# Nine steps of fill products moved from the end of the delta rule's scan to the second group's gram products

## The chip, the cores and the metric

The kernel runs on one core of a Trainium2 chip, as one launch. The metric is the device time of that launch in microseconds (us): the median of three executions is 1509.61 us (1508.7 to 1509.68).

A core has five engines that run side by side, each through its own list of instructions in a fixed order: TensorE (PE in the profile; its weight loads are PEld), VectorE (DVE), ScalarE (ACT), GpSimd (POOL), and SyncE (SP), which here issues most of the transfers (DMAs). An instruction waits on semaphores until what it needs is there, and everything behind it on the same engine waits with it.

## The reference, cut to what matters

One layer works on 512 latent tokens and 256 context tokens of width 1024: a feed-forward block, then two mixers side by side (neighbourhood attention and a gated delta rule, forward and backward over 768 tokens), merged by gates, then a second feed-forward block. The part around the change is the delta rule and the projections of the same normalized input:

```python
qa, ka, va, qkv_b, z_b, a_b, b_b, ga, gb = split_proj(modulate(x, shift_x, scale_x) @ w_in)
...
m = jnp.where(strict, jnp.einsum('...ik,...jk->...ij', k_beta, k) * decay, 0.0)
uw = lax.linalg.triangular_solve(jnp.eye(GDN_CHUNK, dtype=m.dtype) + m, rhs,
                                 left_side=True, lower=True, unit_diagonal=True)
...
def step(s, xc):
    v_new = xc[0] - jnp.einsum('...ck,...kv->...cv', xc[1], s)
    s_next = s * xc[3][..., None, None] + jnp.einsum('...ck,...cv->...kv', xc[2], v_new)
    return s_next, (jnp.einsum('...ck,...kv->...cv', xc[4], s)
                    + jnp.einsum('...cj,...jv->...cv', xc[5], v_new))
```

A unit triangular system per chunk has to be inverted, and a state runs through the chunks in order. The projections qa, ka, va (the attention's) and ga, gb (the merge gates) depend on none of that.

## The kernel before

**The delta rule** works in chunks of 128 tokens: six chunks, each in two directions for four heads. One scan position `s` (0 to 5) holds one forward and one backward chunk; `p` (0 or 1) is a pair of heads. So one call works on four 128x128 blocks: two directions by two heads. The positions go in three groups `bi` of two (s = 0,1; 2,3; 4,5).

For each group:

- `grams(bi)` calls `gram(p, s, ...)` four times. It loads decay rows (`Dt<-gcd`, L1110), subtracts and adds a mask on DVE (L1113), takes the exponential on ACT (L1114), lets PE multiply k by k (and q by k from s = 2 on) in `products` (tile `pq`, recorded at L1049, the line of `mm`), and makes `Bt` (DVE, L1119) and `At` (DVE, L1123). `Bt` goes to memory (`bd<-Bt`, L1120).
- `base_inverse` reads 32x32 diagonal blocks of `bd` back into `L` (`Ltr<-bd` and `L<-bd`, L1139; a copy on ACT, L1140; a memset on POOL, L1142) and inverts all of them at once, 31 pairs of a product and a sum on DVE (`bt`, L1146, and `Xt`, L1147). It writes `rd<-Xt` (L1151). There is one buffer `L`, so the base inverses of the three groups follow each other.
- `inverse(bi, st, ...)` loads `T<-rd` (L1168), transposes it on DVE (L1170, L1171) and joins the blocks to 64 and 128 with small matmuls (tile `pi`).
- `scan_step(p, s, ...)` runs the state: matmuls into `pc` (S by kT, r by Tt, vn by ktail, S by qT, vn by At), with DVE between them (`r`, `vn`, `S`, `otmp`), and additions into `oacc` on POOL (L1289, L1290) for s = 4, 5.

`gdn_out(p)` at the end squares `oacc` on ACT, sums on DVE, takes a root on POOL, scales on DVE (L1303), transposes on PE (L1052) and writes `obd`. Then comes the neighbourhood attention, head pair by head pair (`attend`): scores `sc` (L1433), softmax on DVE and ACT (`pr`, L1441), transposes `pt` (L1448), their copy `pT` on ACT (L1450), and the product with the values (L1459).

**The fills** are 28 products of a 1024x128 weight with the 512 tokens, for qa, ka, va, ga and gb (`FILLS`). Each is cut into FS = 4 steps of six matmuls 128x512 (a weight in a high and a low part: L192, L193, L194, tile `pm`); the last step also copies the result on ACT (`spill`) and sends it to memory (L802). The weight comes by DMA on SP's queue (`wr`, L174), is cast on ACT (`wh`, L137) and its rest is taken on DVE (`wl`, L139). `turn(kind, i)` adds `RATE[kind][i]` to a counter and issues one step for each whole unit, behind the last matmul recorded so far: kind "g" after a gram product, "i" within an inverse, "s" within a scan step, `i` being the group. Before the first gram product stand N0 * FS = 8 steps. After the scan a loop issues steps until `(len(FILLS) - NLATE) * FS` are reached and the last product is whole; what is left is issued behind the first attention head (`for _ in fills`).

**The order on each engine** isn't the order of the program text alone. The kernel is built with `schedule_with_timeline_sim=True`: a planner simulates the engines and puts in the instruction whose inputs are there in its simulation, earlier program text first. A fill step is tied behind one matmul, but a step outside `turn` isn't, and may be drawn forward. On the chip the planned order is fixed, and the times are the chip's.

The order of the program text around the change:

```python
for _ in range(N0 * FS):
    next(fills)
step(grams(0))
base = grams(1)
inv_of(0, 0)
...
while done[0] < (len(FILLS) - NLATE) * FS or done[0] % FS:
    next(fills)
```

Of the kernel before, what the change touches and what calls it, by code (L numbers as in the profile page):

```python
# [58 lines left out]
def body(ctx, tc, I, out, dbg=None):  # L59
# [4 lines left out]
    def pool(name, side="left", space=None):  # L64
        kw = dict(name=name, bufs=1, reuse_waits="tile")
        if space is not None:
            kw["space"] = space
        else:
            kw["side"] = side
        g = tc.tile_pool(**kw)  # L70
        st = ExitStack()
        p = st.enter_context(g)
        return p, st.close
# [492 lines left out]
    g = []  # L566
# [472 lines left out]
    gq, close_gq = pool("gq")  # L1039
    spool, done = [gq], [0]  # L1040
    gb_, close_gb = pool("gbase", "right")
    FS, N0, NKQ, NLATE = 4, 2, 2, 3
    RATE = {"g": (2, 3.9, 0.7), "i": (1.5, 0, 0), "s": (0.7, 0.9, 0.5)}
    NBT, NAT, NT6, NTT = 8, 8, 1, 2

    last = [None]
# [17 lines left out]
    def turn(kind, i):  # L1064

        due[0] += RATE[kind][i]
        while due[0] >= 1:
# [837 lines left out]
```

## Time and profile before

| | before |
|---|---|
| median of 3 executions | 1509.61 us |
| the profiled execution: its own time | 1512.61 us |
| its span in the trace | 1510.8 us |
| PE busy | 1441.6 us (95%) |
| DVE busy | 1149.5 us (76%) |
| ACT busy | 662.8 us (44%) |
| POOL busy | 211.2 us (14%) |
| granted TensorE clock, mean | 0.986 |

The profile is one execution. Times within it run from the start of its span. "Busy" is the time in which an engine has an instruction at work; matmuls are pipelined and their ends are modelled, so the step from one start to the next says more of PE's rate than the length of one. The granted clock is the share of full speed that PE got. In a row of the timeline stand the start, the length, the engine, the line, the operation, the tiles (out<-in), the shapes and the count; in brackets the idle time before it, and what ended that. In the chain of waits each piece is what the next one waited for. The gram products, inverses and scan of the delta rule lie between about 736 and 980 us, and the first attention head follows.

### The profile page before, as it was taken

The numbers are of one execution on the slowest core, as the hardware profiler recorded it, in microseconds if no ns is written. First come the engines' busy times: TensorE is split into PE (matmuls) and PEld (weight loads), VectorE is DVE, ScalarE is ACT, GpSimd is POOL, SyncE is SP. The second block draws the span as 40 slices with busy tenths as digits, with TensorE's granted clock in tenths as the row PEclk, the third lists the DMA queues.
The fourth block names the chain that finished last, engine by engine and source line by source line (L and its number), as shares of the span: only waits on it lengthen the run. The fifth ranks groups of instructions, "written<-read, shape, count | busy, mean of one in ns | idle before, by whom it ended". The sixth has DMA issues, their size and how long they took to land.

```text
span 1510.8 us, 23895 instructions
## 1 busy us (share of the span) xinstructions
PE 1441.6 (95%) x9117; PEld 1262.9 (84%) x9117; DVE 1149.5 (76%) x1975; ACT 662.8 (44%) x1090; POOL 211.2 (14%) x262
## 2 busy tenths in 40 slices
PE   6998999999999989999996998989999999999997
PEld 4778989999997778889875777867778999998886
DVE  8787869999988665778677795567669699886626
ACT  5433524434333386555534334267526454444310
POOL 1000000000000110313201001333221022220001
PEclk9999999999999999999998999999999999999999
DMA  9677664445469444222576514274344143233732
GB/s 375 207 262 232 209 236 171 156 164 167 165 231 397 157 153 134 92 78 91 175 214 183 168 64 124 72 261 146 100 168 144 60 136 107 98 112 121 269 98 83
DMA packets 114948, 248.56 MB, mean 165 GB/s; under 512 B 35145, under 2 KB 50577, under 8 KB 114833
## 3 DMA queue, kind: packets, MB, share of 16 engines
q1 hardware_dynamic: 110192, 229.40, 45.4%
q0 software_dynamic: 3056, 12.33, 2.2%
q10 hardware_dynamic: 1586, 5.32, 0.9%
q8 instruction: 71, 1.16, 0.3%
q14 instruction: 43, 0.35, 0.1%
HBM read 215.50 MB, written 31.50 MB: 163 GB/s over the span
## 4 chain that ended last, share of the span: by engine, by line
PE 69%; DVE 13%; DMA 10%; issue 4%; ACT 3%; POOL 1%; SPq 1%; DVEq 0%; ACTq 0%; POOLq 0%
PE ps L211 15%; PE ps L533 4%; PE ps L535 4%; PE ps L534 4%; PE pm L192 4%; PE pm L193 4%; PE pm L194 4%; PE ps L193 3%; PE ps L192 3%; PE ps L1679 3%; PE ps L194 3%; PE ps L1680 3%; PE ps L1681 3%; PE pc L1049 2%; DVE wl L139 2%
## 5 line engine op out<-in xcount | busy, mean ns | idle before, releaser
L139 DVE TENSOR_TENSOR wl<-wr,wh 128x1024 fp32r<-128x1024 f32 (+1 forms) x184 | 226.8, 1238 | 119.2 <-ACT wh L137 119.0
L137 ACT CAST wh<-wr 128x1024 fp32r<-128x1024 f32 (+1 forms) x184 | 185.9, 1015 | 265.7 <-PE pm L193 60.1
L192 PE MATMUL pm<-uxh,wh 128*128 128x512 f32 x320 | 132.4, 414 | 1.0 <-ACT spill L798 1.0
L194 PE MATMUL pm<-uxh,wl 128*128 128x512 f32 x320 | 127.2, 397 | 0.3 <-DVE wl L139 0.3
L193 PE MATMUL pm<-uxl,wh 128*128 128x512 f32 x320 | 127.1, 397 | 0.0
L211 PE MATMUL ps<-wh,hx 128*128 128x512 f32 x352 | 96.1, 391 | 0.9 <-ACT wh L137 0.9
L211 PEld LDWEIGHTS ps<-wh,hx 128*128 128x128 f32 x352 | 65.9, 188 | 15.3 <-ACT wh L137 1.3
L280 DVE SCALAR_TENSOR_TENSOR adap<-wr,crow 128x1024 f32<-128x1024 f32 x61 | 74.6, 1223 | 2.3 <-DMA wr<-in_w_adaT_dram 1.7
L192 PE MATMUL ps<-uh,wh 128*128 128x256 f32 (+1 forms) x208 | 68.6, 331 | 5.0 <-ACT wh L137 5.0
L194 PEld LDWEIGHTS pm<-uxh,wl 128*128 128x128 f32 x320 | 61.1, 191 | 14.3 <-DVE wl L139 1.3
L192 PEld LDWEIGHTS pm<-uxh,wh 128*128 128x128 f32 x320 | 61.5, 192 | 12.6 <-ACT spill L798 1.4
L193 PEld LDWEIGHTS pm<-uxl,wh 128*128 128x128 f32 x320 | 61.4, 192 | 10.6
L114 POOL TENSOR_TENSOR rs<-ve,mhalf 128x1 f32<-128x1 f32 (+2 forms) x46 | 48.2, 1050 | 140.7 <-DVE ve L110 138.3
L193 PE MATMUL ps<-ul,wh 128*128 128x256 f32 (+1 forms) x208 | 67.5, 326 | 0.0
L194 PE MATMUL ps<-uh,wl 128*128 128x256 f32 (+1 forms) x208 | 66.6, 325 | 0.0
L193 PE MATMUL ps<-uxl,wh 128*128 128x256 f32 (+1 forms) x192 | 61.6, 324 | 2.1 <-DVE uxl L139 2.1
L192 PE MATMUL ps<-uxh,wh 128*128 128x256 f32 (+1 forms) x192 | 60.7, 323 | 1.6 <-ACT uxh L137 1.4
L194 PE MATMUL ps<-uxh,wl 128*128 128x256 f32 (+1 forms) x192 | 61.1, 321 | 0.0
L137 ACT CAST wh<-ra 128x1024 fp32r<-128x1024 f32 x31 | 32.6, 1053 | 58.1 <-PE ps L534 20.2
L533 PE MATMUL ps<-ur,wh 128*128 128x384 f32 x168 | 56.5, 336 | 0.0
L534 PE MATMUL ps<-ur,wh 128*128 128x384 f32 x168 | 56.4, 336 | 0.0
L533 PE MATMUL ps<-uh,wh 128*128 128x384 f32 x168 | 56.4, 336 | 0.0
(498 smaller groups left out, 4264.4 us busy)
## 6 DMA issues: line engine op xcount, KB each, us to landing
wr<-in_w_adaT_dram SPq DMA_DIRECT2D x64, 512.0 KB, 4.8
wr<-in_up_dram SPq DMA_DIRECT2D x56, 512.0 KB, 3.7
wr<-in_win_dram SPq DMA_DIRECT2D x52, 512.0 KB, 3.4
wr<-in_dn_dram SPq DMA_DIRECT2D x51, 512.0 KB, 4.0
ra<-in_up_dram SPq DMA_DIRECT2D x24, 512.0 KB, 4.2
rb<-in_up_dram SPq DMA_DIRECT2D x18, 512.0 KB, 3.3
ra<-in_w_adaT_dram SPq DMA_DIRECT2D x16, 512.0 KB, 5.0
wr<-in_w_o_dram SPq DMA_DIRECT2D x8, 512.0 KB, 4.5
```

Source lines behind the costliest of these rows:

```text
L114: G.tensor_tensor(rs[:], ve[:], mhalf[:, 0:n], ALU.pow)
L137: S.copy(hi, src)
L139: marks["lo"] = V.tensor_tensor(lo, src, hi.bitcast(F32), ALU.subtract).ins
L192: T.matmul(ps, a, uh[:, k, :], start=(k == 0), stop=False)
L193: T.matmul(ps, a, ul[:, k, :], start=False, stop=False)
L194: marks["mm"] = T.matmul(ps, b, uh[:, k, :], start=False, stop=(k == nk - 1)).ins
L211: T.matmul(banks[t][d][:, c0:c1], a[:, sl], b[:, d * 512 + c0:d * 512 + c1], start=first and j == 0, stop=last and j == 2)
L280: V.scalar_tensor_tensor(pr[:], raw[:], 1.0, crow, op0=ALU.mult, op1=ALU.mult, accum_out=col[:, c:c + 1])
L533: T.matmul(ps[:], a, mh, start=k == 0, stop=False)
L534: T.matmul(ps[:], a, ml, start=False, stop=False)
L535: T.matmul(ps[:], b, mh, start=False, stop=k == 3)
L1679: T.matmul(ps[:], a, uh[:, k], start=k == 0, stop=False)
```

## The change

Two constants change. The rate of fill steps after a gram product of the second group goes from 3.9 to 5 for each of its eight turns, and the number of products that may be left for later goes from 3 to 2. No operation is added or removed; steps of the fill list are issued at other places of the program text.

```diff
-    FS, N0, NKQ, NLATE = 4, 2, 2, 3
-    RATE = {"g": (2, 3.9, 0.7), "i": (1.5, 0, 0), "s": (0.7, 0.9, 0.5)}
+    FS, N0, NKQ, NLATE = 4, 2, 2, 2
+    RATE = {"g": (2, 5, 0.7), "i": (1.5, 0, 0), "s": (0.7, 0.9, 0.5)}
```

## The prediction

> **What bounds the kernel now.** I read the busy time of every engine by stretches first, then TensorE's timeline around the stretch in which it is empty, then the waits and the chain of waits, to see what ended that emptiness. The question is where TensorE (PE) is empty, and whether work moved into one empty place leaves another behind.
>
> ```profile
> 800.50:804.00 3.50, 0.01 (x1) 0.00 (x0) 2.06 (x3) 1.95 (x1) 0.00 (x0) 1.00 0.74 209
> 804.00:808.00 4.00, 0.00 (x0) 0.00 (x0) 1.97 (x10) 0.63 (x1) 0.15 (x1) 0.69 0.83 147
> 808.00:812.50 4.50, 0.00 (x0) 0.00 (x0) 2.45 (x14) 0.00 (x0) 1.01 (x5) 0.50 0.99 263
> 812.50:816.00 3.50, 3.46 (x46) 2.46 (x50) 3.35 (x15) 1.86 (x5) 2.81 (x6) 0.54 0.17 52
> 816.00:819.50 3.50, 3.50 (x74) 2.69 (x76) 3.34 (x9) 1.29 (x2) 0.80 (x2) 1.00 0.48 155
> ```
>
> The columns are the stretch, its length, then busy time and instructions of PE, its weight load, VectorE (DVE), ScalarE (ACT) and GpSimd (POOL), the granted clock, the DMA share and GB/s. PE has nothing from 800.5 to 812.5 us, and the clock it gets falls to 0.50 and is still 0.54 up to 816.
>
> ```profile
> 794.81 0.48 PE L192 MATMUL pm<-uxh,wh 128*128 128x512 f32 x1
> 800.12 0.39 PE L194 MATMUL pm<-uxh,wl 128*128 128x512 f32 x1
> 812.54 0.69 PE L1049 MATMUL pi<-T,Bt 32*32 32x32 f32 x32 [12.04 <-DMA T<-rd]
> PE pi L1049 <- DMA T<-rd: 15.2, 3, 12.0
> 800.78 0.70 DVE Xt L1147
> 802.90 4.11 SPq L1151 DMA_DIRECT2D rd<-Xt  x4
> 808.76 3.43 DMA T<-rd
> ```
>
> The first two rows are the first and the last of the 24 matmuls behind the second group's last gram product, then comes the first inverse, 12.04 us after. Of all PE's waits in the scan this is the largest (12.0 of the 15.2 us that PE spent on T<-rd). What it waits for is told by the last rows, of the chain and of SP's queue: DVE ends the first base inverse at 801.48, Xt goes out to memory, and T comes back by 812.19. So 10.7 us of that hole is a round trip that no matmul can shorten; PE can only be given something to do meanwhile.
>
> **What the change does to the order.** The NLATE part does nothing. The loop behind the scan runs until done reaches (28-NLATE)*4 and is a multiple of 4. Counting the due counter through the code, the turns have made 101 steps by then before the change and 110 after: both lie past 100, and both values of NLATE lead to 104 before and 112 after. What acts is the rate 3.9 to 5 on eight turns: they issue 3,4,4,4,4,4,4,4 steps before and eight times 5 after, so 47 become 56 by the first inverse: nine steps more, of six matmuls each. All turns behind it issue the same number as before, each nine steps further on in the list. What is missing at the end is one step of the loop (3 become 2) and all 8 steps, two products, that stood behind the first attention head.
>
> **The front.** Nine steps are 54 matmuls. The two rows above give (800.12-794.81)/23 = 0.231 us from one to the next, so 12.5 us. PE's fills then end at 800.51+12.5 = 813.0 instead of 800.51, and the first inverse starts 0.5 later than 812.54 if T is there by then. In return there is no cold start: in 812.50 to 816.00 PE worked 3.46 us at 0.54, which at full clock is 1.9, so 1.6 us come back. The front is worth **-1.1**.
>
> The moved steps bring their own work along: 2.25 weights, each with a load of 512 KB in SP's queue, a cast on ACT, a split on DVE and a spill at its end.
>
> ```profile
> 795.16 1.22 DVE L139 TENSOR_TENSOR wl<-wr,wh 128x1024 fp32r<-128x1024 f32 x1
> 787.65 1.05 PE L1049 MATMUL pq<-kT 128*128 128x128 f32 x8
> 793.64 1.12 DVE L1119 SCALAR_TENSOR_TENSOR Bt<-pq,beta,Dt 128x128 f32<-128x128 f32 x4
> 799.46 0.68 DVE At L1123
> ```
>
> The splits are 2.25 x 1.22 = 2.7 us on DVE ahead of the end of the first base inverse. Against it, the last Bt and At (1.12 and 0.68) move behind that end, since their products come later. Between +2.7 and -1.8 on T I take 0: PE arrives at 813.0 and T at 812.2, so 0.8 of it is covered anyway, and the rest costs PE one for one. The loads and spills pass the same queue as rd and T; their density per PE time does not change, only its length, so I take 0 there too.
>
> **The second base inverse.** The last Bt of the second group waits for a product that now has seven more steps in front of it: 7 x 6 x 0.231 = 9.7 us, from 788.70 to 798.4. Behind that Bt are its way to memory, the loads of L, ACT's copy, and the second base inverse.
>
> ```profile
> 801.76 1.95 ACT L1140 COPY L<-Ltr 64x1024 f32<-64x1024 f32 x1 [3.93 <-DMA Ltr<-bd]
> 806.81 0.15 POOL L1142 MEMSET L<- 128x32 f32 x1 [46.91 <-DMA L<-bd]
> 853.73 0.69 DVE L1269 COPY S<-pc 128x512 f32<-128x512 f32 x1 [1.92 <-PE pc L1049]
> 832.71 1.14 DVE L1113 SCALAR_TENSOR_TENSOR Dt<-Dt,gcum,cst 128x128 f32<-128x128 f32 x4 [2.85 <-DMA Dt<-gcd]
> 866.88 0.43 PE L1049 MATMUL pi<-T,Bt 32*32 32x32 f32 x26 [0.46 <-DMA T<-rd]
> ```
>
> ACT's copy is done at 803.71, and L is complete only at 806.8: 3.1 us of slack. DVE made that Bt 4.9 us after its product. If it comes at once, at 798.4 instead of 793.64, the second base inverse starts 4.8-3.1 = 1.7 us later; if DVE keeps its distance, 9.7-3.1 = 6.6 later. The inverse that needs it stands at 866.88, where PE waits already. But DVE stood still for 1.92 and 2.85 us between, the 1.92 just ahead of that base inverse's last steps and on PE's account. A start 1.7 later fits into these, so I take the near end and put **0**, and keep up to +4.7 (6.6-1.92) for the range.
>
> **The end.** Here are the places that the nine steps leave.
>
> ```profile
> 964.43 0.69 DVE L1257 TENSOR_TENSOR vn<-pc,beta 128x512 f32<-128x512 f32 x1 [1.14 <-PE pc L1049]
> 965.05 0.48 PE L192 MATMUL pm<-uxh,wh 128*128 128x512 f32 x1
> 969.45 1.05 PE L1049 MATMUL pc<-vn,At 128*128 128x128 f32 x8
> 971.50 1.26 PE L1052 MATMUL pc<-ident,oacc 128*128 128x128 f32 x8
> 972.51 0.48 PE L192 MATMUL pm<-uxh,wh 128*128 128x512 f32 x1
> 977.82 0.39 PE L194 MATMUL pm<-uxh,wl 128*128 128x512 f32 x1
> 979.96 0.66 PE L1052 MATMUL pc<-ident,oacc 128*128 128x128 f32 x4 [1.15 <-DVE oacc L1303]
> 980.54 0.39 PE L1433 MATMUL sc<-kah,qah 64*128 64x256 f32 x2
> 982.27 0.50 PE L192 MATMUL pm<-uxh,wh 128*128 128x512 f32 x1
> 987.87 1.03 PE L1448 MATMUL pt<-ident,pr 128*128 128x128 f32 x8
> ```
>
> The first fill is 24 matmuls around the last At product ((969.45-965.05)/0.231 = 19 of them ahead of it); the second lies between the two pairs' transposes, the third between the first scores and the transposes of their softmax. So the two products written behind the first head are drawn forward into places where PE had to wait: with the second fill in place PE still waits 1.15 for oacc. Taking it away leaves the wait. At the first, the planner put 19 matmuls before At although vn was ready at 965.12; 18 will still be there to put (a turn's six and two steps of the loop), so At gains 0.2, which DVE's own order hides. At the third, the chain is not PE's either:
>
> ```profile
> 984.30 0.68 ACT L1441 ACTIVATE pr<-sc,nm 128x512 f32<-128x512 f32 x1
> 987.53 0.69 DVE L1478 SCALAR_TENSOR_TENSOR ob<-z,ob 128x512 f32<-128x512 f32 x1 [2.14 <-DMA z<-zd]
> 988.26 0.62 ACT L137 CAST obh<-ob 128x512 fp32r<-128x512 f32 x1 [1.32 <-DVE ob L1478]
> 992.31 0.59 ACT L1450 COPY pT<-pt 128x512 f32<-128x512 f32 x1
> ```
>
> The softmax was ready at 984.98, its transposes ran at 987.87, 2.9 later, but ACT fetched them only at 992.31, since casts that wait for DMA stand before the copy. What does go is a delay on POOL:
>
> ```profile
> 972.12 0.74 POOL L1289 TENSOR_TENSOR oacc<-oacc,otmp 128x256 f32<-128x256 f32 x1 [1.40 <-DVE otmp L1288]
> 972.82 1.72 POOL L1290 TENSOR_TENSOR oacc<-oacc,otmp 128x256 f32<-128x256 f32 x1
> 972.59 1.35 DVE L139 TENSOR_TENSOR wl<-wr,wh 128x1024 fp32r<-128x1024 f32 x1 [0.54 <-ACT wh L137]
> ```
>
> POOL's second addition took 1.72 where its twin took 0.74, while DVE split a weight of the last fill beside it. That split now stands earlier: -1.0 on the chain to the transposes. Against it the emptied place (from 972.76 on, over 5 us of fills) is long enough to lose the clock:
>
> ```profile
> 843.58 1.12 PE L1049 MATMUL pi<-Tt,Y 64*64 64x64 f32 x16 [2.58 <-DVE Y L1217]
> 843.60:847.00 3.40, 3.40 (x22) 2.80 (x23) 3.40 (x9) 0.76 (x2) 0.00 (x0) 0.50 0.67 219
> ```
>
> After 2.58 us without work PE got half its clock for over 3 us. The first 12 of the 24 scores between 980.54 and 982.27 then take 0.87 us more. The end is worth -1.0+0.87 = **-0.1**. The sum is -1.1+0-0.1 = -1.2: the profiled execution (span 1510.8, its own time 1512.61) would become 1511.4, and the median, 3.0 us below it, 1509.61-1.2 = **1508.4**. About 0.2%, 3.0 us, is what a measurement of this kernel tells from no change, so the forecast is: nothing to be measured. PE's empty time moves from the front to the end.
>
> **The rivals.** (A) *The end gives back what its fills delayed.* It holds if the planner lets waiting work forward: the last At right behind its own turn's six matmuls, at 966.4 instead of 969.45 (-3.0), the POOL addition (-1.0), the softmax transposes at 985.0 instead of 987.87 (-2.9), these now at half clock (+1.0, as after the 2.58 us above). With the front that is -7.0: **1502.6**. For it: vn and pr were ready that early. Against it: ACT's queue behind DMA at 988 to 992. The Trainium skill, TensorE: Matmul & The Clock Gate, Part 1, says that the clock is halved after at least one idle window of about 3.4 us. By that the last place, some 2.7 us long (982.27 to 984.98), would stay warm and A would be, as an estimate, 1 us faster; the 2.58 us row speaks against it.
>
> (B) *The second base inverse comes late.* Place: the last Bt, and L behind it. It decides once that Bt is over 3.1 us later than 793.64. With DVE's distance to PE kept, the inverse at 866.88 comes 6.6-1.92 = 4.7 later, all behind it too: 1509.61+4.7-0.1 = **1514.2**. For it: DVE was 4.9 behind PE there. Against it: the idle DVE time quoted.
>
> (C) *The hole moves and isn't filled*: the change doesn't do what it says. If DVE keeps its old order, At at 799.46 waits for the product ahead of the 794.81 row, which eight extra steps (48 x 0.231 = 11.1 us) shift to about 806.0. At stands in front of the base inverse's last steps, which ended 801.48-799.46 = 2.0 us behind its start: now 808.0, 6.5 later, and T with it: 1509.61+6.5-0.1 = **1516.0**. Against it: the order is planned anew.
>
> **How the numbers follow.** Forecast 0.45, A 0.26, B 0.20, C 0.06, else 0.03. The forecast alone spans 1506.6 to 1512.6, by the unknowns on T and the clock. A reaches from there to 1502.6, with a little below 1502; B and C above. From 1502 to 1515.5 about 2 in 10 are left out. Faster by over 0.2%: A and 0.05 of the forecast, 0.31; slower: B and C, 0.26; within: 0.43.
>
> **What would show it.** The front is right if PE runs without a break past 812 and the first inverse starts at 813 to 814 at full clock; C if a hole over 4 us stands before it. The second base inverse is right if PE waits under 2 us for T<-rd near 867; B if it waits 4 or more. The end is right if PE is empty for about 5 us before the last transposes and the softmax copy still comes 11 to 13 us after the first scores; A if scores or copy come 5 us sooner. The forecast fails if any one of these carries over 4 us.

## The result, and the profile after

The changed kernel takes 1525.73 us (median of 4 runs, 1522.10 to 1529.64), beside 1509.15 us of the kernel before (4 runs, 1505.78 to 1509.68). The ratio is 1.0115, with a 95% interval of 1.0085 to 1.0145. It is 16.6 us slower, where the forecast of 1508.4 had it a little faster, and lies outside the forecast range of 1502.0 to 1515.5. The profiled execution took 1526.55 us, with a span of 1524.8 and a mean granted clock of 0.981.

These rows of the two timelines place the loss: the first and the last row of the first feed-forward stage, before and then after.

```profile
1201.34 0.28 PE L1679 MATMUL ps<-uxh,wh 128*128 128x256 f32 x1
1371.55 0.28 PE L1680 MATMUL ps<-t14l,bh 128*128 128x256 f32 x1
```

```profile
1211.56 0.28 PE L1679 MATMUL ps<-uxh,wh 128*128 128x256 f32 x1
1385.48 0.28 PE L1680 MATMUL ps<-t14l,bh 128*128 128x256 f32 x1
```

Of the 14.0 us between the spans, 10.2 are there when the stage begins, and 3.7 arise in it (173.9 instead of 170.2 us). Behind it nothing is added. So the scan is the place to look. Here are the rows of PE, DVE and POOL that answer to the hole of before, and then those of SP's queue, all of the changed kernel.

```profile
813.23 0.45 PE L1049 MATMUL pi<-T,Bt 32*32 32x32 f32 x32
823.08 0.65 PE L1049 MATMUL pi<-Y,T 32*32 32x32 f32 x32 [6.65 <-DVE Y L1190]
...
802.16 1.12 DVE L1119 SCALAR_TENSOR_TENSOR Bt<-pq,beta,Dt 128x128 f32<-128x128 f32 x4
812.88 0.69 DVE L1123 TENSOR_TENSOR At<-pq,Dt 128x512 f32<-128x512 f32 x1 [1.35 <-ACT kq L1093]
821.61 1.14 DVE L1113 SCALAR_TENSOR_TENSOR Dt<-Dt,gcum,cst 128x128 f32<-128x128 f32 x4 [6.44 <-DMA Dt<-gcd]
822.67 0.15 DVE L1146 TENSOR_TENSOR bt<-L,Xt 128x2 f32<-128x2 f32 x1
822.74 0.28 DVE L1190 COPY Y<-pi 128x128 f32<-128x128 f32 x1
...
816.81 0.16 POOL L1142 MEMSET L<- 128x32 f32 x1 [1.38 <-ACT L L1140]
```

```profile
805.63 0.46 SPq L1120 DMA_DIRECT2D bd<-Bt  x1
806.18 2.79 SPq L1168 DMA_DIRECT2D T<-rd  x3
810.27 0.93 SPq L1139 DMA_DIRECT2D Ltr<-bd  x2
811.25 2.57 SPq L1139 DMA_DIRECT2D L<-bd  x2
815.74 0.38 SPq L1110 DMA_DIRECT2D Dt<-gcd  x1
```

The old hole of 12.04 us is filled: PE's fills run through and the first inverse starts at 813.23. But a new hole of 6.65 follows within that inverse, where PE waits for DVE's copy Y. DVE can't make it, because its fixed order has a Dt of the third group ahead of it. There are two Dt buffers; one comes free only with the last At of the second group (812.88; 799.46 before), and SP issues the load at 815.74. Beside it, the last Bt is made at 802.16 (793.64 before). Its way to memory stands in SP's queue among the transfers of the first base inverse, L is complete at 816.97 (before at 806.96), and the second base inverse starts at 822.67 instead of 807.00.

The next two fences show three stretches in the view of windows, before and after. The columns are the stretch, its length, the busy time of PE, its weight load, DVE, ACT and POOL (instructions in brackets), the granted clock, the DMA share and GB/s.

```profile
800.00:825.00 25.00, 12.96 (x158) 9.31 (x157) 18.90 (x67) 9.75 (x18) 4.77 (x14) 0.80 0.59 154
800.00:860.00 60.00, 45.00 (x424) 35.53 (x423) 45.46 (x123) 23.31 (x44) 4.77 (x14) 0.86 0.60 173
860.00:960.00 100.00, 92.66 (x1005) 78.70 (x1004) 71.58 (x196) 37.20 (x91) 13.56 (x24) 0.98 0.30 92
960.00:1020.00 60.00, 54.95 (x391) 43.63 (x390) 36.83 (x56) 33.81 (x72) 23.53 (x30) 0.94 0.56 197
```

```profile
800.00:825.00 25.00, 17.48 (x134) 13.52 (x134) 10.91 (x26) 10.28 (x15) 5.38 (x14) 0.91 0.78 200
800.00:860.00 60.00, 50.94 (x458) 39.71 (x458) 38.16 (x112) 25.03 (x48) 5.38 (x14) 0.94 0.66 187
860.00:960.00 100.00, 87.57 (x943) 74.61 (x942) 74.45 (x197) 38.78 (x93) 11.87 (x21) 0.93 0.32 96
960.00:1020.00 60.00, 49.46 (x338) 41.07 (x337) 38.06 (x65) 27.03 (x60) 23.95 (x30) 0.83 0.46 167
```

PE's idle time is the length less its busy time. From 800 to 860 it falls from 15.0 to 9.1 us, in 860 to 960 it rises from 7.3 to 12.4, and in 960 to 1020 from 5.1 to 10.5. The mean clock in the last two falls from 0.98 to 0.93 and from 0.94 to 0.83. The emptied end costs PE about what the filled front gives; the middle is what comes on top. The first row says why: between 800 and 825 DVE is idle 14.1 us instead of 6.1. **PE's hole was not empty on DVE**: in it DVE worked through the first steps of the second base inverse, and now it stands idle for more than half of that time. The last sum of that base inverse ends the delay:

```profile
857.54 0.69 DVE L1147 TENSOR_REDUCE Xt<-bt 128x16 f32<-128x512 f32 x1
```

```profile
875.80 0.68 DVE L1147 TENSOR_REDUCE Xt<-bt 128x16 f32<-128x512 f32 x1
883.37 0.45 PE L1049 MATMUL pi<-T,Bt 32*32 32x32 f32 x32
```

It comes at 857.54 before and at 875.80 after, and the inverse that needs it moves from 866.88 to 883.37. First scores come at 992.51 instead of 980.54; 48 fill matmuls (11.1 us) that stood behind them stand ahead of them now, and the last scores (1064.4 and 1075.1) still are 10.7 late.

### The profile page after: what moved, and what is told of

The parts are those of the page before. It is cut to its first block, busy times and chain, and to the rows that moved or that the text cites. A ratio compares the mean times of both kernels' runs of the same rounds, so it can differ in the third digit from the quotient of the medians.

```text
span 1524.8 us, 23894 instructions
## 1 busy us (share of the span) xinstructions
PE 1452.2 (95%) x9117; PEld 1271.5 (83%) x9117; DVE 1150.1 (75%) x1975; ACT 662.0 (43%) x1090; POOL 209.6 (14%) x262
## 5 line engine op out<-in xcount | busy, mean ns | idle before, releaser
L211 PEld LDWEIGHTS ps<-wh,hx 128*128 128x128 f32 x352 | 65.9, 188 | 15.2 <-ACT wh L137 1.2
L193 PEld LDWEIGHTS pm<-uxl,wh 128*128 128x128 f32 x320 | 61.1, 191 | 10.5
```

The source lines that it names most:

```text
L193: T.matmul(ps, a, ul[:, k, :], start=False, stop=False)
L211: T.matmul(banks[t][d][:, c0:c1], a[:, sl], b[:, d * 512 + c0:d * 512 + c1], start=first and j == 0, stop=last and j == 2)
```

## The experiments

Three theories: **T1**, Dt of the third group, loaded behind the late last At, stands ahead of the first inverse's Y and of the base inverse. **T2**, the last Bt is late, and with it L and the second base inverse. **T3**, the emptied places at the end cost the time. Ratios are to the kernel before, timed beside each run. The absolute times in the expectations go by its first median of 1509.61 us; beside the runs it took 1509.92 (e1 to e4), 1513.33 (e5 to e8), 1512.70 (e9 to e12) and 1512.85 (e13 to e16), so the ratios are what counts.

**The nine steps behind the last product (e1), and six of them (e4).** Rates and NLATE as before:

```diff
     base = grams(1)
+    for _ in range(9):
+        with tc.issue_after(last[0]):
+            next(fills)
```

> The kernel before (rate 3.9, NLATE 3) with nine fill steps written behind the second group's last gram product instead of between its products, in front of the same first inverse. T1 (the late Dt of the third group stands in front of the first inverse's Y copy) and T2 (the second base inverse gets its L late): neither the last Bt (793.6) nor the last At (799.5) comes later, so the fills run to about 813, the first inverse follows at 813 to 815 with no wait of 6 us for Y, the second base inverse starts near 807, and the time is that of before or up to 4 us below it: 1505 to 1510. T3 (the places emptied at the end cost the time): the end is emptied in the same way as in the changed kernel, so the time stays at 1520 to 1526.

> As the first of these, with six steps behind the last gram product instead of nine. T1 and T2: the fills end at 800.5 + 36 x 0.231 = 808.8, PE then waits some 4 us for T, the second base inverse starts near 807, and the time is within 3 us of before: 1506 to 1511. T3: six of nine steps are taken from the end: 1516 to 1523.

e1: 1514.40 us, ratio 1.0033 (1.0020 to 1.0047). The end is emptied as in the changed kernel, with 10.5 us of idle time on PE from 960 to 1020 in both, and yet two thirds of the loss are gone, so T3 isn't the main cause:

```profile
960.00:1020.00 60.00, 49.48 (x358) 39.96 (x356) 36.12 (x59) 30.62 (x68) 24.90 (x32) 0.83 0.51 179
```

But the time is above what T1 and T2 expected. e4: 1507.93, 0.9986 (0.9971 to 1.0001), as expected of T1 and T2. The second base inverse starts at 809.3 and 809.4.

**The changed kernel with Dt behind Y (e2, and again e15).**

```diff
-            V.scalar_tensor_tensor(Dt[:, m], Dt[:, m], gcum[...], msk, ...)
+            with tc.issue_after(marks["Y6"]) if (p, s) == (1, 4) else nullcontext():
+                V.scalar_tensor_tensor(Dt[:, m], Dt[:, m], gcum[...], msk, ...)
...
-        V.tensor_copy(Y6[:], py[:])
+        marks.setdefault("Y6", V.tensor_copy(Y6[:], py[:]).ins)
```

> The changed kernel, with the subtraction of the third group's second Dt on VectorE put behind the first inverse's Y6 copy. T1: the wait of 6.65 us for Y in the first inverse goes, the first scan product comes near 831 instead of 839.2, and if that is what sets the end, the time is within 3 us of before: 1508 to 1513. T2: L is complete only near 817, so the second base inverse still starts 10 us later than before (817 instead of 807), the inverse at 866.9 of before stays 8 to 10 us late, and the time is 1517 to 1521. T3: nothing changes, 1523 to 1528.

> The changed kernel with the third group's second Dt put behind the first inverse's Y6 copy, once more on the chip of these runs. T1: at least 0.3% below the changed kernel's 1.15 to 1.24%, that is below 0.9%. If Dt is worth nothing: 1.1 to 1.25%.

1521.75 us, 1.0085 (1.0064 to 1.0106), and 1523.77, 1.0078 (1.0062 to 1.0093). Rows of DVE and PE in the first of them:

```profile
817.96 0.16 DVE L1147 TENSOR_TENSOR bt<-L,Xt 128x2 f32<-128x2 f32 x1 [2.90 <-POOL L L1143]
818.23 0.28 DVE L1191 COPY Y<-pi 128x128 f32<-128x128 f32 x1
818.56 0.45 PE L1049 MATMUL pi<-Y,T 32*32 32x32 f32 x32 [2.26 <-DVE Y L1191]
```

The hole of 6.65 shrinks to 2.26 (Y now waits for the base inverse's first step, and that for L), but the second base inverse ends at 874.90, nearly as late as in the changed kernel. T1 is worth some 0.4% (the two ratios of the changed kernel, 1.0115 and 1.0124 below, against 1.0085 and 1.0078), not the whole. The first pair's intervals overlap, the second pair's don't.

**Half a dose (e3).** Rate 4.4, which puts four steps between the products, and five behind the last, as in e1.

> Half a dose: rate 4.4 (four of the nine steps between the gram products) and the other five steps behind the last gram product; all fills of the scan stand otherwise as in the changed kernel. T1: the last At is some 5 us late, Dt's load comes near 806 and lands before the first inverse needs VectorE, so the threshold is not reached: 1506 to 1511. T2: the last Bt is about 5 us late, the second base inverse starts 2 to 5 us after 807, and the time is in proportion: 1511 to 1517. T3: 1520 to 1526.

1514.95 us, 1.0028 (1.0008 to 1.0049). The second base inverse starts at 812.6. The time lies where T2 put it, and no threshold shows; but e1, with no product delayed, gives as much.

**At late alone (e5), and with six and four steps (e11, e12, e16).** In `products`, between the last gram's two products:

```diff
         yield one(0, kT, 0)
         turn("g", s // 2)
+        for _ in range(9 if (p, s) == (1, 3) else 0):
+            with tc.issue_after(last[0]):
+                next(fills)
```

> The kernel before (rate 3.9, NLATE 3) with nine fill steps written between the last two products of the second group: the last Bt comes as before, the last At some 12 us later. T1 (what stands behind the late At, the reload of a Dt of the third group, costs the time): 1517 to 1523. T2 (what stands behind the late Bt, its way to memory, L and the second base inverse, costs the time): the second base inverse starts near 807 to 810 and the time is that of the kernel with nine steps behind the last product, 1511 to 1516.

1511.31 us, 0.9990 (0.9976 to 1.0005): a last At that DVE makes at 816.63 costs nothing, and the emptied end, at PE's 10.3 us of idle time from 960 to 1020, costs no more than the front gains. This holds for a plan in which the third group's Dt (821.99) stands behind the first inverse's Y (820.19) on DVE, and not ahead of it as in the changed kernel; that order is what e2 and e15 test. The timeline of PE and DVE, and the window of the middle:

```profile
820.53 0.65 PE L1049 MATMUL pi<-Y,T 32*32 32x32 f32 x32 [2.71 <-DVE Y L1193]
...
807.43 0.16 DVE L1149 TENSOR_TENSOR bt<-L,Xt 128x2 f32<-128x2 f32 x1 [3.90 <-POOL L L1145]
859.63 0.68 DVE L1150 TENSOR_REDUCE Xt<-bt 128x16 f32<-128x512 f32 x1
```

```profile
860.00:960.00 100.00, 93.92 (x1013) 78.90 (x1012) 69.78 (x196) 38.91 (x92) 12.70 (x24) 1.00 0.33 96
```

With the second base inverse on time (807.43 to 859.63) the middle has 6.1 us of idle time and full clock. T2's place holds. Its number doesn't: 1511.31 lies within 1511 to 1516, but 2 us below the kernel before that was timed beside it (1513.33), and T2 expected it above.

> Six steps between the last two products of the second group, three left at the end. T2: the second base inverse near 807 to 809, the front gains as with nine (PE loses 8 to 11 instead of 19 between 800 and 860), the end loses some 3 us (10.8 instead of 7.5 between 960 and 1020, as with six steps behind the last product) instead of 10: 3 to 6 us below before. T3: with a third of the end kept, a third of the loss goes. T1: as T2, the last At is 8 us late and Dt lies near Y: within 2 us of before.

> Four steps between the last two products, five left at the end. T2: 4 x 6 x 0.231 = 5.5 us of the front's hole are filled, the end keeps both of the places behind the last scan products and loses 0 to 2 us: 2 to 5 us below before. T1 and T3: within 2 us of before.

> Four steps between the last two products of the second group, once more: 0.1 to 0.4% below before, as the first time (0.9977, 0.9961 to 0.9994).

Six steps: 1514.53, 1.0007 (0.9986 to 1.0027), a miss; the second base inverse starts at 807.7 but ends at 864.0, and PE waits 2.50 us for T ahead of the next inverse. Four steps: 1510.78, 0.9977 (0.9961 to 0.9994), and again 1510.73, 0.9986 (0.9976 to 0.9997). This is 2 to 3.5 us below the kernel before, and so below both kernels.

**L late alone (e6).** No fill moved; the loads of L for the second base inverse are tied behind the first inverse's last T load.

```diff
+            with tc.issue_after(marks["T"]) if "T" in marks and "L" not in marks else nullcontext():
                 nc.sync.dma_start(dst, bass.AP(bd.tensor, ...))
```

> The kernel before, no fill moved, with the loads of L for the second base inverse issued on SP's queue only behind the first inverse's T loads. The second base inverse then starts near 815 to 818 instead of 807, as in the changed kernel. T2: 8 to 11 us are lost, 1517 to 1521. T1: the late start is hidden ahead of the inverse at 866.9, 1508 to 1512.

1514.24 us, 1.0010 (0.9993 to 1.0027). This is between the two expectations as absolute times, but only 0.9 us above the kernel before that was timed beside it (1513.33), which is T1's place. What moved stands in the timeline of SP's queue and PE, and in the window of the middle:

```profile
799.42 2.68 SPq L1154 DMA_DIRECT2D rd<-Xt  x4
...
807.60 0.65 PE L1049 MATMUL pi<-T,Bt 32*32 32x32 f32 x32 [9.32 <-DMA T<-rd]
```

```profile
860.00:960.00 100.00, 91.00 (x978) 77.72 (x977) 69.16 (x193) 38.09 (x90) 13.49 (x24) 0.91 0.30 87
```

Here rd goes out at 799.42 instead of 802.90, and the first inverse starts 4.9 us sooner. Of these 3.5 us for rd, 2.1 are there because DVE starts the last sum of the first base inverse sooner (798.67 instead of 800.78); the loads of L, no longer in front of rd, can account only for the rest. The second base inverse starts 8.4 later (815.44) but ends only 3.3 later (860.82), so a late start alone doesn't make a late end. The middle loses: clock 0.91 instead of 0.98, idle 9.0 instead of 7.3. The edit moved two things of opposite sign and doesn't tell the theories apart.

**The base inverse late alone (e9).** No fill and no transfer moved:

```diff
-            V.tensor_tensor(t[:, 0:c, 0:i + 1], L[...], Xt[...], ALU.mult)
+            with tc.issue_after(marks["p0"]) if i == 1 and "p0" in marks else nullcontext():
+                V.tensor_tensor(t[:, 0:c, 0:i + 1], L[...], Xt[...], ALU.mult)
...
+            marks.setdefault("p0", p0c.ins)
```

> The kernel before, no fill and no transfer moved, with the first step of the second base inverse on VectorE put behind the first inverse's L1206 copy, so that it starts near 817 instead of 807 although L is there. The first inverse stays near 812.5. T2: PE loses 7 to 9 us more between 860 and 960 (idle time and lowered clock; 8.5 in the first trace of before, 7.0 in the second), 5 to 9 us above before. T1: nothing, within 2 us of before.

1520.96 us, 1.0047 (1.0028 to 1.0065), that is 7 us:

```profile
814.01 0.70 PE L1049 MATMUL pi<-T,Bt 32*32 32x32 f32 x32 [11.29 <-DMA T<-rd]
882.39 0.65 PE L1049 MATMUL pi<-T,Bt 32*32 32x32 f32 x32 [4.47 <-DMA T<-rd]
...
820.65 0.16 DVE L1147 TENSOR_TENSOR bt<-L,Xt 128x2 f32<-128x2 f32 x1
872.74 0.68 DVE L1148 TENSOR_REDUCE Xt<-bt 128x16 f32<-128x512 f32 x1
```

This is the cleanest run for the last link of T2, the late base inverse: the first inverse is 1.5 us from where it was, the base inverse starts 13.6 us late and ends 15.2 late, and the inverse behind it waits 4.47 us for T. The price is as expected.

**Bt late: nine steps ahead of the last gram (e10), of the last two (e13), of all four (e14).** As e5, with the loop ahead of `yield one(0, kT, 0)`, and the condition (1, 3), (0, 3) or (0, 2).

> The kernel before with nine steps written ahead of the last two products of the second group, so that the last Bt comes 12 us later; against the run with nine steps between these two products it moves one product (8 matmuls) across 54 fill matmuls. T2: the second base inverse starts at 820 or later, PE loses 10 us or more on top of that run between 860 and 960, and the time is 12 to 18 us above before. T1: nothing but Dt counts, which is not planned ahead of Y here: within 3 us of before. T3 (the emptied end): within 3 us of before, since the run with nine steps between the products was there too.

> The kernel before with nine steps ahead of the products of the second group's last two grams. T2 (VectorE has nothing to do in PE's old hole, and the second base inverse ends late): the second base inverse ends at 869 to 876 as in the run with the last gram alone (868.8) or in the changed kernel (875.8); if the work of the earlier grams' Bt and At adds to it, nearer to 876 and 0.5 to 0.9% above before; if only the last Bt counts, 0.2 to 0.4%.

> The kernel before with nine steps ahead of all products of the second group. As the run before, with all eight products 12 us late: 0.8 to 1.3% above before if the earlier grams' work counts, 0.2 to 0.4% if only the last Bt counts. Dt is not planned ahead of Y here: if T1 (Dt ahead of Y) is the rest, 0.2 to 0.4% too.

1.0023 (1.0006 to 1.0040), 1.0053 (1.0034 to 1.0072) and 1.0044 (1.0029 to 1.0059). e10 against e5, which differ by one product, has the sign that T2 wants, but a third of its size or less. The last Bt is made at 802.85, 806.50 and 805.82, and the second base inverse ends at 868.76, 876.97 and 877.16. So delaying the gram ahead of the last one too makes the last Bt and the base inverse later, and e13 lies 0.3% above e10, though the two intervals just overlap. Delaying the first two as well adds nothing (e14 is not above e13, and lies in neither of its two ranges).

**Both kernels once more (e7, e8).**

> The changed kernel once more, for a second trace. In the first one 10.3 us of the difference were there ahead of the first feed-forward stage, and 3.7 arose in it (173.8 us from its first to its last L1679 matmul, 170.1 before). If the 3.7 belong to the kernel, 173.8 stands again; if to the run, it is nearer to 169 or 170, while first scores stay near 992 and the second base inverse near 822. Time 1522 to 1529.

> The kernel before once more, for a second trace and for the scatter between two measurements of one kernel. All theories: the first inverse near 812 to 815, the second base inverse near 807 to 809, first scores near 980, 1507 to 1512, ratio 1.000 within 0.15%. The second trace's positions tell how far two profiles of one kernel lie apart.

The changed kernel: 1531.05 us, 1.0124 (1.0104 to 1.0144); Y is waited for 7.80 us, the second base inverse starts at 826.25. The kernel before: 1514.04, 1.0006 (0.9991 to 1.0021); 806.91, first scores at 977.6. The feed-forward stage takes 174.1 and 170.7 us, so the 3.7 us came back with the kernel. That they belong to it isn't shown: the same stage takes 169.2 to 172.4 us in the runs e1 to e6 and e9 to e16, and 169.2 and 169.5 in e2 and e15, which are the changed kernel but for one Dt.

All runs by one measure, the second base inverse on DVE (its first step and its last sum) and the first matmul of the feed-forward stage:

| | ratio | starts | ends | stage |
|---|---|---|---|---|
| before, first and second trace | 1; 1.0006 | 807.0; 806.9 | 857.5; 856.5 | 1201.3; 1198.0 |
| e12, e16: four steps behind Bt | 0.9977; 0.9986 | 805.5; 807.5 | 858.5; 859.8 | 1195.2; 1200.1 |
| e4, e1: six, nine behind the last product | 0.9986; 1.0033 | 809.4; 809.3 | 863.4; 859.0 | 1197.3; 1199.0 |
| e11, e5: six, nine behind Bt | 1.0007; 0.9990 | 807.7; 807.4 | 864.0; 859.6 | 1203.6; 1201.6 |
| e6: L late | 1.0010 | 815.4 | 860.8 | 1201.3 |
| e3: half a dose | 1.0028 | 812.6 | 864.5 | 1205.9 |
| e10, e13, e14: Bt late | 1.0023; 1.0053; 1.0044 | 817.5; 823.0; 823.5 | 868.8; 877.0; 877.2 | 1203.2; 1208.8; 1208.5 |
| e9: base inverse late | 1.0047 | 820.7 | 872.7 | 1212.5 |
| e2, e15: changed, Dt behind Y | 1.0085; 1.0078 | 818.0; 818.0 | 874.9; 874.1 | 1209.9; 1212.0 |
| changed, first and second trace | 1.0115; 1.0124 | 822.7; 826.3 | 875.8; 881.0 | 1211.6; 1216.5 |

Where the base inverse ends at 868 or later, the stage starts at 1203 to 1217; where it ends by 865, at 1195 to 1206. The end of the base inverse sorts the runs better than the nine steps do, but not cleanly: the two groups overlap at 1203 to 1206, and e1 (859.0, 1.0033) stands above e10 (868.8, 1.0023). (e9's profiled execution took 1525.98, the longest of its ten; its stage is late by as much as 5 us for that.)

**What stays open.** Of the 1.15 to 1.24%, a late last Bt explains 0.2 to 0.5 (e10, e13, e14) and Dt ahead of Y some 0.4 (e2, e15). Between e13 or e14 and e15, 0.3% are left, with the base inverse ending no later; no run names their cause. The traces give a place only: from 860 to 960 PE is idle for 15.0 us in e15, and for 12.1 and 11.1 in e13 and e14; in e15 it waits there mostly for DVE (T, Y and vn), in the other two mostly for T<-rd. Nor is it settled why e1 stands 0.4% above e5, or why e11 gained nothing where four steps did.

## Why the prediction was wrong

**The step that failed is "The second base inverse", where I put 0** (bounds up to +4.7). I let the last Bt come 4.8 to 9.7 us late; it was 8.5 (793.64 to 802.16), so that size was within its bounds. What I didn't price is what stands behind it. Its write reached SP's queue 10.8 later (794.79 to 805.63), L was complete 10.0 later, and Dt then took 5.7 more: a start 15.7 late against my worst case of 6.6. The idle time of DVE that I quoted as cover (1.92 and 2.85) was no cover: DVE's idle time between 825 and 860 is 8.4 us before (35 - 26.56) and 7.8 after (35 - 27.25), both from the differences of the two window rows. The base inverse ended 18.3 late. e9 prices such a delay by itself at 7 us, rival B's place and more than its 4.7. Even this isn't the whole loss: Dt ahead of Y adds some 0.4%, and 0.3% stay open.

My sign for this step was badly chosen. I wrote that it is right if PE waits under 2 us for T<-rd. The inverse at 883.37 starts without any such wait, 16.5 us late, since PE had other work until then. The delay came as waits for DVE around it:

```profile
872.09 1.13 PE L1049 MATMUL pc<-vn,ktail 128*128 128x128 f32 x8 [2.00 <-DVE vn L1257]
885.92 0.42 PE L1049 MATMUL pi<-Y,T 32*32 32x32 f32 x28 [2.10 <-DVE Y L1190]
888.40 0.99 PE L1049 MATMUL pi<-T,Bt 64*64 64x64 f32 x16 [1.73 <-DVE T L1206]
```

**The front** was half right. PE's fills run past 812 and the first inverse starts at 813.23 (I wrote 813 to 814; it is 816.82 in the second trace), with no wait for T in either, so 0 for splits and loads held there. But -1.1 stopped at the first inverse. I followed the late last At only to the first base inverse (rival C) and not to the buffer that it frees: Dt's reload, and Y behind it. The first scan product came 9.0 late (830.22 to 839.19). "The loads pass the same queue, I take 0" failed for this one load.

**The end** cost no more than the front gained in e5, which is what I added up, but by other sizes than mine. POOL's second addition fell from 1.72 to 0.72, and PE waits 4.41 for oacc, about the 5 us that I wrote:

```profile
989.69 0.66 PE L1052 MATMUL pc<-ident,oacc 128*128 128x128 f32 x2 [4.41 <-DVE oacc L1303]
...
985.33 0.72 POOL L1290 TENSOR_TENSOR oacc<-oacc,otmp 128x256 f32<-128x256 f32 x1
```

The softmax copy comes 6.3 us after the first scores (998.79), not 11 to 13, and still nothing is won: last scores follow the first by 82.6 us, 83.9 before. My sign of 11 to 13 us failed here. So did the clock's term: I counted half clock for 12 scores, 0.87 us. The mean clock from 960 to 1020 fell from 0.94 to 0.83, which is, as an estimate from these two rows, 0.11 x 60 / 0.5 = 13 us more at half clock. e5, which has the same end, stands at 0.9990; it shows that front and end together cost nothing there, not that -0.1 was right by itself. Rival A's gain didn't come.

**NLATE** does nothing by the count of steps. No run changed it alone; e1 keeps NLATE at 3, and its end is as empty as the changed kernel's.

So a net of about zero for "PE's hole filled, the end emptied" is what e5 shows, which behaves as I predicted; e1, which delays no product at all, stands 0.3% above before. The change does more than that: it delays the products that the hole's other users wait for.

## What to carry to other kernels

A hole on one engine is seldom a hole on all: before filling it, list what the other engines do in it, and which inputs of theirs stand behind the place where the filling is put. Put the filling behind the product that the others' longest chain waits for (here the one for the last Bt), not ahead of it, and try how much of it pays: of the nine steps nothing clear was gained there (0.9990 and 1.0033), of four 0.1 to 0.2%. And follow each delayed instruction to the buffer that it frees and the load that waits for that buffer. Where each engine runs a fixed order, that load can stand ahead of work that has nothing to do with it.

## What the runs showed of the hardware

The clock fell after a shorter gap than the 2.58 us that I used. Rows of e2: the gap of 2.26 us shown above, then PE's fills and the clock in windows.

```profile
818.50:820.50 2.00, 1.94 (x37) 1.62 (x38) 1.95 (x7) 0.50 (x2) 0.00 (x0) 0.75 0.72 156
820.50:822.50 2.00, 2.00 (x7) 1.52 (x6) 0.77 (x4) 0.00 (x0) 0.00 (x0) 0.50 0.82 284
822.50:824.00 1.50, 1.50 (x37) 1.00 (x36) 0.00 (x0) 0.00 (x0) 0.00 (x0) 0.86 1.04 388
```

If the clock is either 1.00 or 0.50, the shares 0.75 and 0.86 put half clock from 819.5 to 822.9: it sets in about 1 us after PE is back at work (818.56) and lasts 3.4 us. The Trainium skill, TensorE: Matmul & The Clock Gate, Part 1, has the clock halved after at least one idle window of about 3.4 us and says that the windows run freely. The delayed onset and the length of 3.4 us agree with such windows; the gap of 2.26 doesn't agree with a window that has to be idle throughout.

In the first feed-forward stage the matmuls run at two spacings while the clock is shown as 1.00. From the 600th to the 720th matmul of the stage, before and after:

```profile
1278.96 0.28 PE L1679 MATMUL ps<-uxh,sh 128*128 128x256 f32 x1
1292.56 0.28 PE L1679 MATMUL ps<-uxh,wh 128*128 128x256 f32 x1
```

```profile
1290.09 0.28 PE L1679 MATMUL ps<-uxh,sh 128*128 128x256 f32 x1
1304.22 0.28 PE L1679 MATMUL ps<-uxh,wh 128*128 128x256 f32 x1
```

120 matmuls take 13.60 us before and 14.13 after, 113 and 118 ns each. The first trace of before goes at the quicker spacing from about the 480th to the 1200th matmul of the stage, the second from about the 60th to the 780th, and both traces of the changed kernel mostly from the 960th to the 1200th. Other kernels take either spacing too: e1 and e9 go at 118 ns throughout the stage, e5 at 113 through most of it. PE's waits in the stage, most of them for DVE, are 3.2 us instead of 1.8; that leaves 2.3 of the 3.7 us, for which the spacing is the likely place. What sets the spacing was not tried.
